# Bisecting the selection threshold in the float's own bits instead of ordered integers

## The chip, the cores and the metric

The kernel runs on one core of a Trainium2 chip. The metric is the time of one execution on the device, in microseconds (us); the median of several runs counts. The engines are TensorE (PE, with its weight loads as PEld), VectorE (DVE), ScalarE (ACT), GpSimd (POOL) and SyncE (SP), which here issues nearly all DMAs. Each engine works through its own queue in a fixed order and waits on semaphores for the others.

## The reference, cut to what matters

One decoder layer over 1024 tokens of width 1024: a norm, one wide projection, three token mixers (A: sparse attention, B: gated spatial MLP, C: differential attention), a gated merge, an output projection, and a feed-forward part with a final norm. The change touches A's choice of keys: each query keeps the 256 causal keys with the highest indexer score.

```python
score = jnp.einsum('bqh,bqhs->bqs', wb.astype(jnp.float32) * w_scale, jax.nn.relu(dots))
score = jnp.where(causal[None], score, -jnp.inf)
_, sel = lax.top_k(score, top_k)          # top_k = 256
...
logits = jnp.where(valid[:, :, None, :], logits, NEG)
p = jax.nn.softmax(logits, axis=-1).astype(v.dtype)
```

## The kernel before

Tokens are handled in eight tiles of 128 queries. Matmuls run as three products of a high and a low part (`mm`, line 84, over the pairs of `split_pairs`). The first phase, up to some 700 us, holds the projections, B, C, A and the gated merge; then come the output projection and the feed-forward part.

The indexer scores of tiles 2 to 7 lie in SBUF (`scA`, `scB`). No list of keys is built. Instead `selection` looks for each query's 256th highest score by bisection, bit by bit: 32 steps, each over all six tiles. A step makes a candidate threshold for every query and tile (128x6 values), counts in four tiles on VectorE (line 442, is_lt with a sum) and in the two largest on ScalarE (line 439, Sign with a sum), compares the counts with the goal (line 445) and takes the candidate where it holds (line 446, a predicated copy). Floats don't order like integers of the same bits when they are negative, so the candidate is kept as an ordered integer `K`, in which setting a bit makes it larger (line 432), and `to_float` turns it into the float's bits by a shift and mask (line 413) and an XOR (line 414):

```python
nc.vector.tensor_scalar(t, K, 31, INT_MAX, op0=ALU.arith_shift_right, op1=ALU.bitwise_and)
nc.vector.tensor_tensor(f, K, t, op=ALU.bitwise_xor)
```

After the last step the threshold above is tried (lines 453 to 471), and then six masks are made, one per tile (lines 484 to 493). A's softmax reads a mask for tiles 2 to 7; tiles 0 and 1 have a plain causal mask.

The work around it is written as generators that are advanced in turn. The projections of C take one selection step for each half of a product. Then a loop takes one half-step of `c_attention`, one step of `selection`, and one or two steps of `fill`, which holds B, A's projections, the gates of A, A's values (`proj_v`), and branches b and c. After C the selection is finished, then A runs with two steps of `fill` for each of its own. C works head by head (four heads): its Q and K come as two tiles each (`cQ`, `cK`) and V as one (`cV`), all from a ring of six places (tag `stk`), which A's `aQ`, `aK1`, `aK2`, `aV` use after them. C's score matmuls are line 576, its row minima on VectorE line 538, transposes line 510, value products line 525. A's scores are lines 795 and 796.

The order that an engine ends up with is not this order: the framework reorders each engine's queue by a simulated timeline when it builds the program, so a changed instruction can move others far away.

Of the kernel before, what the change touches and what calls it, by code (L numbers as in the profile page):

```python
# [12 lines left out]
I32 = mybir.dt.int32  # L13
AF = mybir.ActivationFunctionType
ALU = mybir.AluOpType

P = 128
# [9 lines left out]
INT_MIN = -(2 ** 31)  # L27
# [9 lines left out]
def trunk_kernel(tc, x, attn_g, w_in, ikg, ikb, sgug, sgub, sguw, sgubs, dlam, dsub,  # L37
                 wba, wbb, wbc, w_out, mlp_g, w_ff1, w_ff2, fin_g, out):
    nc = tc.nc
# [4 lines left out]
    with ExitStack() as top:  # L44
# [12 lines left out]
        def small(shape, name, bufs=4, dtype=F32):  # L57
            return spool[0].tile(shape, dtype, name=name, tag=name, bufs=bufs)
# [78 lines left out]
        with ExitStack() as ph:  # L137
# [61 lines left out]
            for i in range(NT):  # L199
# [3 lines left out]
                if i == 0:  # L203
# [7 lines left out]
                    for s in range(2):  # L211
# [4 lines left out]
                        for k0, kn, (H, L) in cv_parts:  # L216
                            a, b = max(k0, 4 * s), min(k0 + kn, 4 * s + 4)
# [94 lines left out]
            for i in range(NT):  # L312
                nc.vector.tensor_scalar(ikn[:, i, :], ikn[:, i, :], mv[:, i, 0:1], ikrs[:, i:i + 1],
                                        op0=ALU.subtract, op1=ALU.mult)
# [89 lines left out]
            NQ = len(QT)  # L404
# [3 lines left out]

            def to_float(K, tag):

                t = small([P, NQ], "selt", 2, I32)
                f = small([P, NQ], tag, 2, I32)
                nc.vector.tensor_scalar(t, K, 31, INT_MAX, op0=ALU.arith_shift_right, op1=ALU.bitwise_and)
                nc.vector.tensor_tensor(f, K, t, op=ALU.bitwise_xor)
                return f

            def sjunk(i):
                return (sja if i in ON_ACT else sjd)("junk")

            def selection():  # L420


                for a, i in enumerate(QT):
                    nc.vector.memset(thr[:, a:a + 1], float(P * (i + 1) - TOPK * (2 if i in ON_ACT else 1)))
                K = small([P, NQ], "selK", 1, I32)
                nc.vector.memset(K, INT_MIN)
                for b in range(31, -1, -1):
                    cand = small([P, NQ], "selc", 2, I32)
                    if b == 31:
                        nc.vector.memset(cand, 0)  # L430
                    else:
                        nc.vector.tensor_scalar(cand, K, 1 << b, None, op0=ALU.bitwise_or)
                    f = to_float(cand, "self")
                    cnt = small([P, NQ], "selcnt", 2)
                    for a, i in enumerate(QT):
                        junk = sjunk(i)
                        th = f[:, a:a + 1].bitcast(F32)
                        if i in ON_ACT:
                            nc.scalar.activation(junk[:, 0:P * (i + 1)], sc[i], AF.Sign, bias=th, scale=-1.0,
                                                 accum_out=cnt[:, a:a + 1])  # L440
                        else:
                            nc.vector.tensor_scalar(junk[:, 0:P * (i + 1)], sc[i], th, None,  # L442
                                                    op0=ALU.is_lt, op1=ALU.add, accum_out=cnt[:, a:a + 1])
                    ge = small([P, NQ], "selge", 2, I32)
                    nc.vector.tensor_tensor(ge, cnt, thr, op=ALU.is_le)
                    nc.vector.copy_predicated(K, ge, cand)
                    yield

                lo = small([P, NQ], "sello", 1, I32)
                hi_ = small([P, NQ], "selhi", 1, I32)  # L450
# [13 lines left out]
                for a, i in enumerate(QT):  # L464
                    if i in ON_ACT:
                        junk = sjunk(None)
                        nc.vector.tensor_scalar(junk[:, 0:P * (i + 1)], sc[i], f1[:, a:a + 1].bitcast(F32), None,
                                                op0=ALU.is_ge, op1=ALU.add, accum_out=cnt[:, a:a + 1])
                ge = small([P, NQ], "selge", 2, I32)
# [375 lines left out]
            def run_all(g):  # L845
                while next(g, 0) is None:
                    pass

            sel = selection()

            PER, count = 2, [0]
# [477 lines left out]
```

## Time and profile before

| | |
|---|---|
| median of 3 runs | 1477.47 us |
| lowest, highest | 1473.58, 1477.86 us |
| profiled execution | 1471.62 us |
| its span in the profile | 1469.9 us |
| mean granted clock of TensorE | 0.986 |
| busy: PE, PEld | 1414.8, 1195.9 us |
| busy: DVE, ACT, POOL | 998.6, 706.5, 566.7 us |

The profile is one execution. Busy times are those of the engine's instructions; matmuls are pipelined, so that a record lasts longer than the distance to the next, and their ends are modelled. The selection's counts run from 100 to 380 us, its masks until 440 us.

### The profile page before, as it was taken

The numbers are of one execution on the slowest core, as the hardware profiler recorded it, in microseconds if no ns is written. First come the engines' busy times: TensorE is split into PE (matmuls) and PEld (weight loads), VectorE is DVE, ScalarE is ACT, GpSimd is POOL, SyncE is SP. The second block draws the span as 40 slices with busy tenths as digits, with TensorE's granted clock in tenths as the row PEclk, the third lists the DMA queues.
The fourth block names the chain that finished last, engine by engine and source line by source line (L and its number), as shares of the span: only waits on it lengthen the run. The fifth ranks groups of instructions, "written<-read, shape, count | busy, mean of one in ns | idle before, by whom it ended". The sixth has DMA issues, their size and how long they took to land.

```text
span 1469.9 us, 20626 instructions
## 1 busy us (share of the span) xinstructions
PE 1414.8 (96%) x7257; PEld 1195.9 (81%) x7257; DVE 998.6 (68%) x2012; ACT 706.5 (48%) x1314; POOL 566.7 (39%) x373
## 2 busy tenths in 40 slices
PE   7999999998999999999999799999998699999997
PEld 6988888787978888887999578888887587888886
DVE  7478999999996644311615884444443799889795
ACT  6366667677533544422203565555544434334354
POOL 5102341112034323445522134444442557465574
PEclk9999999999999999999999899999999899999999
DMA  8446352535465657464633334444443944543522
GB/s 261 116 122 202 112 167 68 175 86 153 128 195 165 179 148 221 132 221 131 211 122 115 115 136 158 158 151 154 144 144 121 342 157 154 209 146 130 196 66 115
DMA packets 145344, 228.79 MB, mean 156 GB/s; under 512 B 16212, under 2 KB 79064, under 8 KB 145240
## 3 DMA queue, kind: packets, MB, share of 16 engines
q1 hardware_dynamic: 145240, 227.47, 47.7%
q8 instruction: 57, 0.93, 0.3%
q14 instruction: 47, 0.39, 0.1%
HBM read 152.46 MB, written 74.97 MB: 155 GB/s over the span
## 4 chain that ended last, share of the span: by engine, by line
PE 77%; DVE 12%; DMA 6%; issue 2%; ACT 1%; SPq 1%; POOL 0%; POOLq 0%; DVEq 0%; ACTq 0%
PE mm L84 29%; PE ff L1139 19%; PE fo L1292 17%; PE mm L994 4%; PE O L525 2%; DMA w2raw<-in_w_ff_dram 2%; DVE junk L442 2%; PE tp L510 1%; PE tp L994 1%; SPq L53 1%; DVE aS L1241 1%; DMA wr<-in_w_in_dram 1%; DVE cE L538 1%; DMA aK<-ak 1%; PE S L576 1%
## 5 line engine op out<-in xcount | busy, mean ns | idle before, releaser
L1292 PE MATMUL fo<-w2S,aS 128*128 128x512 f32 x1344 | 309.2, 392 | 18.0 <-ACT w2S L1240 15.5
L1139 PE MATMUL ff<-HS,WS 128*128 128x512 f32 x1344 | 312.0, 394 | 4.5 <-ACT WS L1020 1.6
L1292 PEld LDWEIGHTS fo<-w2S,aS 128*128 128x128 f32 x1344 | 254.1, 189 | 73.1 <-ACT w2S L1240 18.7
L1139 PEld LDWEIGHTS ff<-HS,WS 128*128 128x128 f32 x1344 | 253.3, 189 | 63.2 <-ACT WS L1020 2.4
L77 POOL TENSOR_TENSOR wl<-wr,wh 128x1024 fp32r<-128x1024 f32 x48 | 118.3, 2466 | 345.4 <-ACT wh L76 287.9
L84 PE MATMUL mm<-hH,wh 128*128 128x512 f32 (+1 forms) x544 | 214.3, 394 | 5.0 <-ACT gt L709 1.9
L84 PE MATMUL mm<-hH,wl 128*128 128x512 f32 (+1 forms) x544 | 212.6, 391 | 0.0
L84 PE MATMUL mm<-hL,wh 128*128 128x512 f32 (+1 forms) x544 | 212.2, 390 | 0.0
L1241 POOL TENSOR_TENSOR w2S<-w2raw,w2S 128x512 fp32r<-128x512 f32 x80 | 123.5, 1569 | 116.2 <-ACT w2S L1240 116.2
L1240 ACT CAST aS<-araw 128x512 fp32r<-128x512 f32 x112 | 62.5, 618 | 160.9 <-PE fo L1292 120.6
L1021 POOL TENSOR_TENSOR WS<-wraw,WS 128x1024 fp32r<-128x1024 f32 x35 | 85.2, 2435 | 138.8 <-ACT WS L1020 133.5
L1241 DVE TENSOR_TENSOR aS<-araw,aS 128x512 fp32r<-128x512 f32 x112 | 128.6, 1194 | 5.2 <-ACT aS L1240 5.2
L84 PEld LDWEIGHTS mm<-hH,wh 128*128 128x128 f32 x544 | 102.7, 189 | 26.3 <-ACT gt L709 3.4
L84 PEld LDWEIGHTS mm<-hH,wl 128*128 128x128 f32 x544 | 102.6, 189 | 19.9
L84 PEld LDWEIGHTS mm<-hL,wh 128*128 128x128 f32 x544 | 102.8, 189 | 18.6
L1296 DVE TENSOR_TENSOR x3b<-x3b,fo 128x512 f32<-128x512 f32 x168 | 106.7, 676 | 9.1 <-PE fo L1292 9.0
L76 ACT CAST wh<-wr 128x1024 fp32r<-128x1024 f32 x48 | 50.3, 1048 | 110.5 <-PE mm L84 47.0
L736 DVE SCALAR_TENSOR_TENSOR gt<-gt,mm 128x512 f32<-128x512 f32 x32 | 21.8, 683 | 72.5 <-PE mm L84 60.0
L544 ACT ACTIVATE cE<-cE,cEm 128x128 f32<-128x128 f32 (+7 forms) x64 | 49.6, 778 | 35.1 <-DVE cEm L541 18.8
L519 ACT CAST ptH<-tp 128x512 fp32r<-128x512 f32 (+1 forms) x80 | 42.6, 543 | 39.4 <-PE tp L510 31.9
L520 DVE TENSOR_TENSOR ptL<-tp,ptH 128x512 fp32r<-128x512 f32 (+1 forms) x80 | 50.2, 631 | 11.6 <-ACT ptH L519 10.1
L442 DVE TENSOR_SCALAR_CACHE_REDUCE junk<-scA,self 128x512 bf16<-128x512 f32 x64 | 55.8, 871 | 0.3
(309 smaller groups left out, 2873.6 us busy)
## 6 DMA issues: line engine op xcount, KB each, us to landing
wr<-in_w_in_dram SPq DMA_DIRECT2D x42, 512.0 KB, 4.6
araw<-a_s SPq DMA_DIRECT2D x28, 768.0 KB, 4.3
wraw<-in_w_ff_dram SPq DMA_DIRECT2D x16, 1024.0 KB, 5.3
a_s<-s SPq DMA_DIRECT2D x64, 256.0 KB, 2.0
a_s<-a SPq DMA_DIRECT2D x48, 256.0 KB, 2.3
w2raw<-in_w_ff_dram SPq DMA_DIRECT2D x8, 1536.0 KB, 8.0
araw<-a_s SPq DMA_DIRECT2D x14, 512.0 KB, 3.7
t_b<-gt SPq DMA_DIRECT2D x24, 256.0 KB, 2.9
```

What stands on the lines that cost most here:

```text
L76: nc.scalar.copy(H, raw)
L77: nc.gpsimd.tensor_tensor(L, raw, hi(H), op=ALU.subtract)
L84: nc.tensor.matmul(ps, st, mv, start=(i == 0), stop=(i == n - 1))
L442: nc.vector.tensor_scalar(junk[:, 0:P * (i + 1)], sc[i], th, None, op0=ALU.is_lt, op1=ALU.add, accum_out=cnt[:, a:a + 1])
L520: nc.vector.tensor_tensor(L[:, 0:w], tpf[:, 0:w], hi(H[:, 0:w]), op=ALU.subtract)
L994: nc.tensor.matmul(ps, st_, mv_, start=(kh == 0 and n_ == 0), stop=(kh == 1 and n_ == len(prs) - 1))
L1021: eng.tensor_tensor(W[:, 1], src, hi(W[:, 0]), op=ALU.subtract)
L1139: nc.tensor.matmul(ps, s_, mv_, start=(n in (1, 5, 2) and m_ == 0), stop=(m_ == len(prs) - 1), skip_group_check=True)
L1240: nc.scalar.copy(t[:, 0, i], s_[:, i])
L1241: eng.tensor_tensor(t[:, 1, i], s_[:, i], hi(t[:, 0, i]), op=ALU.subtract)
L1292: nc.tensor.matmul(ps, s_, mv_, start=(n in (1, 2, 5) and m_ == 0), stop=(m_ == len(prs) - 1), skip_group_check=True)
L1296: nc.vector.tensor_tensor(xs, xs, ps, op=ALU.add)
```

## The change

The threshold is kept as the float's own bits. The start is -1, all bits set, which is what `to_float` makes of the smallest integer. The first candidate is 0, as before. From then on the candidate of a bit is `K` XOR that bit: in a positive float the bit is set, which makes it larger; in a negative one, whose bits start all set, it is cleared, which makes it larger as well. Only after the 32 steps `to_float`, which is its own inverse, turns `K` into an ordered integer once, into a tile of its own (`selKo`), and the rest reads that. Of a step's six small instructions on VectorE two are no longer there; the counts now read the candidate `selc` and not `self`. Line numbers behind line 425 are higher by one, behind line 448 by two.

```diff
                 K = small([P, NQ], "selK", 1, I32)
-                nc.vector.memset(K, INT_MIN)
+                nc.vector.memset(K, -1)
                 for b in range(31, -1, -1):
-                    cand = small([P, NQ], "selc", 2, I32)
+                    f = small([P, NQ], "selc", 2, I32)
                     if b == 31:
-                        nc.vector.memset(cand, 0)
+                        nc.vector.memset(f, 0)
                     else:
-                        nc.vector.tensor_scalar(cand, K, 1 << b, None, op0=ALU.bitwise_or)
-                    f = to_float(cand, "self")
+
+                        nc.vector.tensor_scalar(f, K, 1 << b, None, op0=ALU.bitwise_xor)
                     cnt = small([P, NQ], "selcnt", 2)
...
                     nc.vector.tensor_tensor(ge, cnt, thr, op=ALU.is_le)
-                    nc.vector.copy_predicated(K, ge, cand)
+                    nc.vector.copy_predicated(K, ge, f)
                     yield
+                K = to_float(K, "selKo")
```

The build also moves other instructions. Three places:

VectorE, one of the first steps of the bisection, in the order before (`stL` is the low part of a projection, not of the selection):

```order
L445 TENSOR_TENSOR selge<-selcnt,selthr 128x6
L446 COPY_PREDICATED selK<-selge,selc 128x6
L432 TENSOR_SCALAR selc<-selK 128x6
L413 TENSOR_SCALAR selt<-selc 128x6
L345 TENSOR_TENSOR stL<-mm,stH 128x512
L414 TENSOR_TENSOR self<-selc,selt 128x6
L442 TENSOR_SCALAR junk,selcnt<-scB,self 128x384
L442 TENSOR_SCALAR junk,selcnt<-scA,self 128x512
```

The pair of lines 413 and 414 stands between the candidate and its counts. In the order of the changed kernel:

```order
L446 TENSOR_TENSOR selge<-selcnt,selthr 128x6
L447 COPY_PREDICATED selK<-selge,selc 128x6
L434 TENSOR_SCALAR selc<-selK 128x6
L443 TENSOR_SCALAR junk,selcnt<-scB,selc 128x384
L345 TENSOR_TENSOR stL<-mm,stH 128x512
L443 TENSOR_SCALAR junk,selcnt<-scA,selc 128x512
```

The two instructions of `to_float` are gone, and the first count follows the candidate directly.

SP, the loads for C's last head (heads are counted from 0, so head 3), in the order before: `wr` of 128x8x128 are a gate's weights, `wr` of 128x4x256 half of the weights for A's values, `t_a` and `o_s` are stores:

```order
L53 DMA o_s_1550<-ot 128x2x64
L53 DMA cK<-ck_1084 32x1024
L53 DMA cK<-ck_1085 32x1024
L53 DMA cQ<-cq_1080 32x1024 x2
L53 DMA cQ<-cq_1081 32x1024 x2
L53 DMA wr<-in_w_in_dram 128x8x128
L53 DMA wr<-in_w_branch_b_dram 128x2x128
L53 DMA wr<-in_w_in_dram 128x4x256
```

The gate's weights stand behind the C loads. In the changed kernel:

```order
L53 DMA t_a_77<-gt 128x512
L53 DMA wr<-in_w_branch_b_dram 128x2x128
L53 DMA wr<-in_w_in_dram 128x8x128
L53 DMA cK<-ck_1084 32x1024
L53 DMA cK<-ck_1085 32x1024
L53 DMA cK<-ck_1084 32x1024
L53 DMA cK<-ck_1085 32x1024
L53 DMA cQ<-cq_1080 32x1024 x2
L53 DMA cQ<-cq_1081 32x1024 x2
L53 DMA wr<-in_w_in_dram 128x4x256
```

The gate's weights stood behind the C loads and now stand in front of them; half of the weights for A's values takes the place behind.

TensorE, from the last score matmul of head 2 on, in the order before; the first row is the last that reads head 2's second Q tile, whose place in the ring the second K tile of head 3 takes (21 more matmuls of line 84, one of line 681 and two of line 600 follow before a score with that tile, 128x128):

```order
L576 MATMUL S_4383<-cK_3624,cQ_3623 128x512
L576 MATMUL S_4533<-cK_4510,cQ_4509 128x128
L525 MATMUL O_4144<-ptL_4164,cV_3633 128x256
L525 MATMUL O_4144<-ptH_4163,cV_3633 128x256
L525 MATMUL O_4144<-ptL_4164,cV_3633 128x256
L525 MATMUL O_4144<-ptH_4175,cV_3633 128x256
L525 MATMUL O_4144<-ptL_4176,cV_3633 128x256
L525 MATMUL O_4144<-ptH_4175,cV_3633 128x128
L525 MATMUL O_4144<-ptL_4176,cV_3633 128x128
L84 MATMUL mm_4738<-hH_110,wh_4610 128x512
L84 MATMUL mm_4738<-hL_112,wh_4610 128x512
L84 MATMUL mm_4738<-hH_110,wl_4611 128x512
```

A gate's product begins behind the value products. In the changed kernel, where the first row is the last reader of that place and the last row the first score with the new tile:

```order
L578 MATMUL S<-cK,cQ 128x512
L578 MATMUL S<-cK,cQ 128x128
L84 MATMUL mm<-hH,wl 128x512
L527 MATMUL O<-ptL,cV 128x256
L527 MATMUL O<-ptH,cV 128x256
L527 MATMUL O<-ptL,cV 128x256
L512 MATMUL tp<-ident,cE 128x128 x3
L683 MATMUL mm<-vn,wsT 128x256
L527 MATMUL O<-ptH,cV 128x256
L683 MATMUL mm<-vn,wsT 128x256 x2
L578 MATMUL S<-cK,cQ 128x128
```

The 24 matmuls of a gate's product no longer stand between the last reader and the new tile's first score.

## Rows read from the trace of the kernel before

**Rows 1.** Page, part 1: engine, busy us, share, instructions.
```profile
PE 1414.8 (96%) x7257; PEld 1195.9 (81%) x7257; DVE 998.6 (68%) x2012; ACT 706.5 (48%) x1314; POOL 566.7 (39%) x373
```

**Rows 2.** Busy time by stretches: us, then PE, PEld, DVE, ACT, POOL; clock, DMA share, GB/s.
```profile
106.00:441.00 335.00, 324.82 (x1854) 278.51 (x1852) 317.11 (x998) 213.29 (x445) 74.92 (x48) 0.99 0.49 142
...
441.00:634.00 193.00, 190.83 (x1011) 162.64 (x1010) 99.83 (x273) 85.91 (x182) 76.30 (x69) 1.00 0.54 164
```

**Rows 3.** Chain of waits: start us, duration us, what; two of its pieces.
```profile
320.43 0.60 PE tp L510 x4
...
855.00 277.01 PE ff L1139 x1210
```

**Rows 4.** TensorE groups by shape, 106 to 441 us; last what ended the idle time.
```profile
L84 PE MATMUL mm<-hH,wh 128*128 128x512 f32 x269 | 107.0, 398 | 5.0 <-ACT gt L709 1.9 <-DVE yt L691 1.6 <-DVE stL L345 1.1
...
L84 PE MATMUL mm<-wh,hH 128*128 128x256 f32 x192 | 55.0, 286 | 0.0
...
L510 PE MATMUL tp<-ident,cE 128*128 128x128 f32 x144 | 23.2, 277 | 0.0
...
L576 PE MATMUL S<-cK,cQ 128*128 128x512 f32 x48 | 18.8, 409 | 0.2 <-DVE cEm L538 0.2
...
L525 PE MATMUL O<-ptL,cV 128*128 128x256 f32 x64 | 18.0, 298 | 1.2 <-DVE ptL L520 1.0
```

**Rows 5.** VectorE groups, 106 to 441 us: line, shapes, count, busy us, mean ns, idle before.
```profile
L432 DVE TENSOR_SCALAR selc<-selK 128x6 int32<-128x6 int32 x31 | 7.4, 240 | 0.5
...
L414 DVE TENSOR_TENSOR self<-selc,selt 128x6 int32<-128x6 int32 x31 | 5.4, 174 | 0.5
...
L413 DVE TENSOR_SCALAR selt<-selc 128x6 int32<-128x6 int32 x31 | 5.2, 168 | 0.6
```

**Rows 6.** VectorE timeline of one step: start us, duration us, instruction.
```profile
245.11 0.17 DVE L413 TENSOR_SCALAR selt<-selc 128x6 int32<-128x6 int32 x1
...
245.31 0.17 DVE L414 TENSOR_TENSOR self<-selc,selt 128x6 int32<-128x6 int32 x1
...
246.05 0.16 DVE L586 RECIPROCAL cr<-cEs 128x1 f32<-128x1 f32 x1
...
246.13 0.40 DVE L646 SCALAR_TENSOR_TENSOR u<-gsq,mm 128x256 f32<-128x256 f32 x1
```

**Rows 7.** Chain of waits, start of the A stretch.
```profile
397.66 5.72 DMA aK<-ak
...
448.34 0.23 PE S L796
```

**Rows 8.** Chain of waits around the late weight.
```profile
326.64 6.14 DMA wr<-in_w_in_dram
...
334.71 7.20 PE mm L84 x24
```

**Rows 9.** TensorE timeline, 331 to 335 us; idle time and its releaser in brackets.
```profile
331.04 0.45 PE L576 MATMUL S<-cK,cQ 128*128 128x512 f32 x2
...
332.51 0.28 PE L525 MATMUL O<-ptL,cV 128*128 128x128 f32 x1
...
334.71 0.80 PE L84 MATMUL mm<-hH,wh 128*128 128x512 f32 x1 [1.92 <-ACT gt L709]
```

**Rows 10.** Stretch behind the late weight; columns as in rows 2.
```profile
334.70:338.10 3.40, 3.39 (x8) 2.71 (x9) 2.14 (x9) 3.37 (x9) 2.30 (x2) 0.53 0.86 257
```

**Rows 11.** SP timeline: the loads of head 3's second key.
```profile
331.46 1.72 SPq L53 DMA_DIRECT2D cK<-ck  x4
```

**Rows 12.** View of the tile cK: all its 32 loads.
```profile
DMA to landing us min/median/max: 2.3/3.2/5.5
```

**Rows 13.** VectorE groups of the masks, 385 to 441 us.
```profile
L488 DVE TENSOR_TENSOR_SCAN pf<-seleq,cm 128x384 f16<-128x384 bf16 (+5 forms) x6 | 10.0, 1663 | 0.0
...
L489 DVE SCALAR_TENSOR_TENSOR seleq<-pf,selneed,seleq 128x384 bf16<-128x384 f16 (+5 forms) x6 | 5.7, 948 | 0.1
```

## What was predicted

> **What bounds the kernel now.** I read the page first, then the busy time of each engine by stretches, then the groups of instructions inside the stretch that the change touches, then single places on the timeline and the chain of waits. The page says that TensorE is shown busy for 1414.8 of 1469.9 us and VectorE for 998.6 us [rows 1]. Taken over the whole span VectorE looks idle for a third of the time, but the change lies in one stretch, from the first candidate to the masks, 106 to 441 us. There VectorE is busy for 317.1 of 335 us, and TensorE for 324.8 [rows 2]. Behind that stretch VectorE falls to 99.8 of 193 us while TensorE stays at 190.8 [rows 2]. So in the stretch both engines are nearly full, and neither is free to give back what the other saves.
>
> TensorE's shown idle time of 10.2 us there is a lower bound, because the ends of matmuls are modelled. In the plain matmul run of the first feed-forward product 1210 matmuls of 512 columns take 277.01 us, 0.229 us each [rows 3]. In the stretch there are 856 of 512 columns (three groups of line 84, of which one is shown, and 48 scores) and 736 of 256 (three groups of line 84, 128 of line 525, 32 others) [rows 4]. At 0.229 us and half of that they need 196 and 84 us. The 144 records of transposes cost 0.15 us each by the chain, 21.6 us [rows 3, 4], and I allow 13 us for what is small. That is 315 of 335 us: an estimate of 20 us of gaps, 10.2 of them visible. These 20 us are all that this stretch can give, whatever VectorE saves.
>
> **The change part by part.** *The removed pair.* Each of the 32 steps loses a shift-and-mask (line 413) and an XOR (line 414); one pair of the 32 ran in the start-up, before VectorE had other work. The 31 pairs of the stretch are busy for 5.2 and 5.4 us, 10.6 us [rows 5]. Bounds: where the next instruction needs the result, the starts lie 0.20 us apart (245.11, 245.31), where it doesn't, about 0.08 us (246.05 to 246.13, a reciprocal) [rows 6]. 62 times these is 12.4 and 5.0 us. Since the scheduler puts other work between some of them and none between others, I take the 10.6 us.
>
> [...]
>
> *The OR that becomes an XOR* (line 432, 240 ns on average [rows 5]) keeps its form, one source and one constant on 128x6 integers: nothing. The memsets (-1 for the smallest integer) run in the start-up: nothing. *The conversion at the end* adds one pair behind the last step, 0.3 us at the same durations, taken once. Net for VectorE: 10.3 us less, so 306.8 of work for 335 us.
>
> *The moved instructions.* The order of every engine changes from the first C tiles on. Up to the second matmul of the first masked A score (448.34 us in the chain of before [rows 7]), VectorE has the same work as before less 62 instructions, two of them of the start-up and the new pair counted against the removed ones. But TensorE has 64 more 512-column matmuls in front of that place (1026 of line 84 against 962), 64 x 0.229 = 14.7 us of filling work that before stood behind it. On VectorE the six masks begin after 75 of the 96 C score chunks, not after 92, and end after 92, not after 96. So selection and masks go ahead of the last C tiles, and gates and projections on TensorE fill for them. The amount of TensorE work in the kernel stays the same, 7257 matmuls. So what the time can gain is only what gaps it loses.
>
> *The late weight.* On SP the load of a gate's weights stands behind C loads for the next head, which wait for tiles of the head in front: it is on its way from 326.64 for 6.14 us, and then it is copied and split [rows 8]. [...]
>
> *A new wait at the last head.* The tile of head 3's second key goes into the place of head 2's second query. In before that place is read last at 331.04 [rows 9], SP issues the four loads from 331.46 on for 1.72 us, and a load lands a median of 3.2 us after its issue, 2.3 to 5.5 [rows 11, 12]: ready some 4.9 us after the last read starts. TensorE's queue has 6.9 us of work between that last read and the first use (24 matmuls of 512 columns, seven value products and a few small ones), so nothing waits. In the new order 1.8 us of work stand there: one of 512 columns, a score of 128, seven of 256 and three transposes. So TensorE waits about 4.9 - 1.8 = 3.1 us. [...] By the same reckoning over all loads of Q, K and V tiles, the other short cover, 4.8 us for a key tile of A's third head, is the same in both orders.
>
> *VectorE's own part of the gaps.* In the rows of TensorE's groups [rows 4] 6.4 us of idle time stand (5.0, 1.2, 0.2), and VectorE ends 1.6, 1.1, 1.0 and 0.2 of it, 3.9 us or 61%; ScalarE's 1.9 is the late weight. The same share of 20 us is 12.2 us. VectorE's free time in the stretch goes from 17.9 to 28.2 us, and TensorE has 14.7 us of other work to put into what is left. I take two thirds, 8.1 us, as gained; bounds are 0 and 12.2.
>
> *What is late next.* In the A stretch 14.7 us of filling work are missing; it has 2.2 us of visible gaps in 193 us [rows 2]. I take a loss of 1.4 us there, with bounds 0 and 5.7, the length of one key load of A in the chain of before [rows 7]. TensorE's last 3834 of 7263 rows, from branch c on, stand in the same order as before.
>
> **Sum.** 8.1 + 3.6 - 4.8 - 1.4 = 5.5 us gained. The profiled execution took 1471.6 us (1469.9 of span and 1.7 around it), so 1466.1 by its own level. The median of the three runs shown is 1477.5, 5.9 us above it; at that level, which is the one that I give, the forecast is 1477.5 - 5.5 = 1472.0 us.
>
> **Rivals.**
> *TensorE stays the bound.* Both engines are in-order queues that feed each other, and TensorE has 315 of 335 us of work in the stretch. If its gaps come from the weaving (a transpose, a copy by ScalarE, a subtraction by VectorE, and back) and not from VectorE's load, VectorE merely gets idle time, as it has behind 441 us [rows 2]. For it: 94% use of TensorE in the stretch. Against it: VectorE is at 95% there and named for most visible gaps. The time is then between 1473 and 1481 us, about 1477.
>
> *The masks in front of the C tiles* (slower). The two costliest lines of the masks are busy for 15.7 us [rows 13], the six masks with all their lines for some 35. Before, they had nearly all of C behind them. Now the last 21 C chunks stand among and behind them in VectorE's queue, and TensorE's queue holds the transposes and value products of these tiles in a fixed place. TensorE's cover up to the last C score is 48 more matmuls of 512 columns (11.0 us) and 30 of 256 (3.4 us). If the masks' 35 us push C past that cover, TensorE waits 35 - 14 = 21 us; less the 5.5 that the forecast gains it is 15 us slower, 1493 us. It is slower by over 0.3% once TensorE waits more than 9.9 us there. Against it: the masks are interleaved chunk by chunk with C and not in one block, and waits of this sort, of TensorE on VectorE, are short in before, 1.0 us on the value products of line 525 [rows 4].
>
> *The pair is not removed, only renamed.* The built order has 3 of the 34 shift-and-masks left, so this gets hardly any chance.
>
> **How the numbers follow.** Changes below about 0.3%, 4.4 us, can't be told from none on this kernel. The forecast gets 0.58 and spans 2 to 18 us gained, 1459 to 1475; 0.55 of it lies past the 4.4 us and 0.03 short of them. TensorE as the bound gets 0.25, within 0.3% on either side. The masks get 0.15, all counted as slower. The renaming gets 0.02 (same). So faster 0.55; same 0.03 + 0.25 + 0.02 = 0.30; slower 0.15. The likeliest is 1472.0 us. Low end 1459: nearly all of the 20 us of gaps go, with no new wait. High end 1481: all of the bound's case. What is left out is some 0.04 below and 0.15 above.
>
> **What would show it.** VectorE's lines 413 and 414 fall from 34 instructions each to 3, and its busy time by about 10 us. In the stretch up to the first masked A score VectorE's busy share falls below 0.95, and TensorE's gaps shrink: the whole place should come at about the same time as before (441 to 450 us), with 64 more matmuls done. No gate weight should be waited for near 330 us, but TensorE should wait some 3 us for a key tile of head 3 at its first score with it. If the place comes at 455 us or later, TensorE was the bound. If TensorE waits at transposes of C's exponentials while VectorE runs lines 486 to 495, the masks' rival is right. The forecast is wrong, too, if the new order brings a new late load in the A stretch.

## The result and the profile of the changed kernel

The changed kernel is slower: 1488.15 us (median of six runs, 1485.29 to 1491.49) against 1474.93, ratio 1.0094 with an interval of 1.0075 to 1.0112. Timed again beside later experiments it took 1494.48 us, ratio 1.0136 (1.0115 to 1.0157). So it loses some 14 to 20 us where 5.5 were to be gained. The two timings of this one kernel lie 0.42% apart, 6.2 us, more than their intervals tell, so a difference of a few us between two experiments is safe only where the traces show it too. The profiled execution took 1489.2 us with a span of 1487.5.

Page of the changed kernel, part 1, as in [rows 1]:

```profile
PE 1420.3 (95%) x7257; PEld 1197.5 (81%) x7257; DVE 990.7 (67%) x1950; ACT 704.9 (47%) x1314; POOL 574.1 (39%) x373
```

Busy time by stretches, columns as in [rows 2]: the two stretches of before, and 3.4 us at a new wait.

```profile
106.00:441.00 335.00, 317.68 (x1797) 271.65 (x1796) 309.86 (x935) 208.00 (x438) 75.40 (x47) 0.99 0.49 140
441.00:634.00 193.00, 190.01 (x1002) 160.16 (x1001) 97.70 (x270) 84.64 (x181) 71.87 (x66) 1.00 0.55 163
340.40:343.80 3.40, 3.34 (x8) 2.67 (x9) 3.33 (x13) 1.75 (x6) 1.91 (x1) 0.53 0.97 254
```

VectorE works 7.9 us less in all. But between 106 and 441 us TensorE is busy for 317.7 us instead of 324.8. What it waits for there, and on to 500 us (engine and line, what was waited for, us in total, times, longest):

```profile
PE mm L84 <- DVE gv L648: 3.0, 1, 3.0
PE mm L84 <- DVE u L648: 1.9, 1, 1.9
PE S L578 <- DMA cV<-cvs: 1.9, 1, 1.9
PE mm L84 <- DVE gt L738: 1.7, 1, 1.7
PE O L527 <- DVE ptL L522: 1.6, 3, 0.8
PE mm L84 <- DVE selneed L488: 1.6, 1, 1.6
PE mm L683 <- DVE u L685: 1.4, 1, 1.4
PE mm L84 <- POOL wl L77: 1.2, 1, 1.2
```

In before the longest wait of this stretch was 1.92 us, for the late weight [rows 9]. Six of these eight lines are waits for VectorE, the engine that was relieved.

Where the time goes can be read from one long unbroken piece of TensorE's work near the end of each chain of waits: 1210 matmuls of the first feed-forward product, and the last 927 of the second. In the chain of the changed kernel (start us, duration us, what):

```profile
868.57 277.01 PE ff L1141 x1210
...
1266.15 210.88 PE fo L1294 x927
```

In before the first of them begins at 855.00 [rows 3], the second at 1247.88:

```profile
1247.88 212.47 PE fo L1292 x927
```

So the changed kernel is 13.6 us late before the feed-forward part, and loses 4.7 us more inside it, some 800 us behind the last instruction that was edited.

### The profile page after: what moved, and what is told of

It is laid out like the page before. It is cut to its first block, busy times and chain, and to the rows that moved or that the text cites. A ratio compares the mean times of both kernels' runs of the same rounds, so it can differ in the third digit from the quotient of the medians.

```text
span 1487.5 us, 20573 instructions
## 1 busy us (share of the span) xinstructions
PE 1420.3 (95%) x7257; PEld 1197.5 (81%) x7257; DVE 990.7 (67%) x1950; ACT 704.9 (47%) x1314; POOL 574.1 (39%) x373
## 4 chain that ended last, share of the span: by engine, by line
PE 70%; DVE 16%; DMA 6%; issue 4%; ACT 2%; POOL 1%; SPq 1%; POOLq 0%; DVEq 0%; ACTq 0%
PE mm L84 27%; PE ff L1141 19%; PE fo L1294 14%; PE mm L996 3%; DMA w2raw<-in_w_ff_dram 2%; DVE junk L443 2%; PE O L527 2%; DVE cE L540 2%; PE tp L512 1%; DVE aS L1243 1%; DMA wr<-in_w_in_dram 1%; DVE x3b L1298 1%; PE tp L996 1%; DVE cE L590 1%; DMA wr<-in_w_branch_c_dram 1%
## 5 line engine op out<-in xcount | busy, mean ns | idle before, releaser
L1294 PE MATMUL fo<-w2S,aS 128*128 128x512 f32 x1344 | 309.9, 393 | 20.4 <-ACT w2S L1242 14.9
L77 POOL TENSOR_TENSOR wl<-wr,wh 128x1024 fp32r<-128x1024 f32 x48 | 120.7, 2516 | 359.8 <-ACT wh L76 327.9
L1243 POOL TENSOR_TENSOR w2S<-w2raw,w2S 128x512 fp32r<-128x512 f32 x80 | 127.4, 1617 | 118.0 <-ACT w2S L1242 118.0
L84 PEld LDWEIGHTS mm<-hL,wh 128*128 128x128 f32 x544 | 103.0, 189 | 18.6
L84 PE MATMUL mm<-wh,hH 128*128 128x256 f32 x192 | 55.3, 288 | 4.5 <-DVE gv L648 3.0
```

The costliest lines, as they stand in the source:

```text
L77: nc.gpsimd.tensor_tensor(L, raw, hi(H), op=ALU.subtract)
L84: nc.tensor.matmul(ps, st, mv, start=(i == 0), stop=(i == n - 1))
L1243: eng.tensor_tensor(t[:, 1, i], s_[:, i], hi(t[:, 0, i]), op=ALU.subtract)
L1294: nc.tensor.matmul(ps, s_, mv_, start=(n in (1, 2, 5) and m_ == 0), stop=(m_ == len(prs) - 1), skip_group_check=True)
```

## The experiments

Two theories stood first. O: the rebuilt order of the queues costs the time. R: the removal itself does (counts that start earlier push other work back). To tell them apart a kernel needs one kernel's arithmetic and the other's order. This addition does that; the table `_ORDER` (left out here) holds, for each engine, the instructions by their place in the traced program, in the order wanted:

```python
for order in json.loads(zlib.decompress(base64.b64decode(_ORDER))).values():
    for a, b in zip(order, order[1:]):
        tc.add_manual_dep(ins[b], ins[a].name,
                          _mb.DependencyInfo(_mb.DependencyClass.NoSync, _mb.DependencyReason.DATA), reason="order")
```

These are order edges without a wait. "Order held" below means this.

**Changed arithmetic, order of before** (e1). The diff of the change, with the order held to that of before; the one conversion stands behind the last step.

> The changed arithmetic (32 pairs of small VectorE instructions gone, one pair added), with every engine's queue held in the order of the kernel before. Theory O (the rebuilt order costs the time): without the new order this is no slower than before; if VectorE's load is part of TensorE's gaps, as forecast, it gains some 8 us (1467), if TensorE is the bound it gains 0 to 3 us (1472 to 1475). Theory R (the removal itself costs: the counts start earlier and push other work of VectorE and ScalarE back): the order does not matter, and this takes what the changed kernel takes, about 1488 us.

Measured: 1470.40 us (12 runs), ratio 0.9968 (0.9954 to 0.9983). Theory R falls: in the order of before the removal gains 4.7 us, 0.32% of 1475. Its chain:

```profile
854.88 277.01 PE ff L1141 x1210
...
1247.12 210.88 PE fo L1294 x927
```

**Arithmetic of before, new order** (e2). No edit but the order, held to that of the changed kernel.

> The arithmetic of before (all 32 pairs), with every engine's queue held in the order of the changed kernel, each pair directly behind its candidate. Theory O: as slow as the changed kernel or somewhat slower, 1488 to 1496 us, since the 62 instructions (10.6 us of VectorE) come on top of the new order. Theory R: as fast as before, about 1475 us.

Measured: 1502.88 us, ratio 1.0188 (1.0162 to 1.0213). The order alone costs 28 us with the pairs in, and the pairs cost 8 to 15 us in it (against the two timings of the changed kernel). That is 7 us above the range expected, but Theory O stands.

**The pair twice, order of before** (e3).

```diff
                 nc.vector.tensor_tensor(f, K, t, op=ALU.bitwise_xor)
+                if tag == "self" and steps[0] < 32:
+                    steps[0] += 1
+                    nc.vector.tensor_scalar(t, K, 31, INT_MAX, op0=ALU.arith_shift_right, op1=ALU.bitwise_and)
+                    nc.vector.tensor_tensor(f, K, t, op=ALU.bitwise_xor)
                 return f
```

> Before, with the pair done twice in each of the 32 steps (64 instructions more, some 11 us of VectorE), every queue otherwise in the order of before. This is the price of the pair in a fixed order. If VectorE's load sets TensorE's gaps, as forecast: slower by 8 to 11 us, 1483 to 1486. If TensorE is the bound and VectorE's small instructions lie beside its work: within 3 us of before.

Measured: 1492.20 us, ratio 1.0123 (1.0101 to 1.0145): 18 us slower, 6 us above the higher of the two expectations. VectorE's busy time rises by more than the 11 us that were added, from 998.6 to 1019.3 us, since a few small instructions became much longer: the new lines 419 and 420 take 260 and 305 ns on average, the pair of before 168 and 174 [rows 5], while their medians are 172 and 166 ns and their longest 2.3 and 2.4 us. What these long ones fall together with is shown in the last section. TensorE's waits, 106 to 440 us:

```profile
PE O L531 <- DVE ptL L526: 5.1, 4, 2.7
PE mm L84 <- DVE gv L652: 3.6, 1, 3.6
PE S L582 <- DMA cK<-ck: 3.5, 1, 3.5
```

So in one and the same order 64 small instructions more cost 18 us and 62 fewer gain 5. VectorE's busy time goes up by 20.7 us in the one case and down by 5.0 in the other (993.6 us in e1); a second trace of before (e0) shows 1000.5, so a difference of 2 us says little.

**Short counts, order of before** (e5). On top of e1, VectorE's counts see only the first 128 keys, with a goal of 64. It leaves out the other keys of four tiles, so the masks are others.

```diff
-                    nc.vector.memset(thr[:, a:a + 1], float(P * (i + 1) - TOPK * (2 if i in ON_ACT else 1)))
+                    nc.vector.memset(thr[:, a:a + 1], float(P * (i + 1) - 2 * TOPK) if i in ON_ACT else 64.0)
...
-                            nc.vector.tensor_scalar(junk[:, 0:P * (i + 1)], sc[i], th, None,
+                            nc.vector.tensor_scalar(junk[:, 0:P], sc[i][:, 0:P], th, None,
```

> The changed arithmetic in the order of before, and VectorE's four counts of each step read only the first 128 keys instead of 384 to 768 (their goal is 64, so that the threshold is another and so is the output). That takes some 57 us of work from VectorE without moving an instruction. If VectorE's load set TensorE's gaps, as forecast (61% of 20 us): 8 to 12 us below the changed arithmetic in the order of before (1470), 1458 to 1462. If TensorE's gaps in this order come from the weaving of the queues: 0 to 4 us below, 1466 to 1470.

Measured: 1464.21 us, ratio 0.9935 (0.9914 to 0.9956), 4.9 us below e1 by the ratios. Its first feed-forward piece begins at 850.78 us, 4.1 before e1's. VectorE's busy time falls by another 59.9 us, to 933.7, and brings what the 5.0 of the pairs brought. Neither expectation is hit; the pairs and the shorter counts together, 65 us of VectorE's load, gave some 10 us, about half of the 20 us of gaps.

**Two sets of instructions moved up in VectorE's queue** (e4, e7). Each queue held, but in the new order five instructions, and in e1's order six, stand a few places earlier. The first of e4's five:

```
+L648 SCALAR_TENSOR_TENSOR gv<-gsq,mm 128x256
 L434 TENSOR_SCALAR selc<-selK 128x6
 L443 TENSOR_SCALAR junk,selcnt<-scB,selc 128x384
 L443 TENSOR_SCALAR junk,selcnt<-scA,selc 128x512
-L648 SCALAR_TENSOR_TENSOR gv<-gsq,mm 128x256
```

> The changed kernel in its own order, with five instructions moved up in VectorE's queue alone, each a few places: two of line 648 ahead of counts (line 443), one of line 685 ahead of two row minima and a predicated copy, one of line 252 ahead of a mask's scan (line 490), one of line 738 ahead of the small instruction of line 622. In the changed kernel TensorE waits for these five 3.0, 1.9, 1.4, 1.6 and 1.7 us, though their inputs are there earlier. Theory Q (the new order costs because VectorE's queue puts bulk in front of results that TensorE waits for): gains 3.0 + 1.6 + 0.8 + 1.5 + 1.7 = 8.6 us, 1479 to 1482. Theory S (VectorE is full in the new order, so that TensorE's waits only show its surplus of work): the waits come back at the next places, at most 3 us gained, 1485 to 1488.

Measured: 1492.70 us, ratio 1.0128 (1.0109 to 1.0148), above both ranges: nothing gained. The five waits are gone (lines 685 and 738, and 648 near 340 us) or shorter (0.3 and 0.9 us). Others stand at other places (e4's waits of TensorE, 106 to 500 us; the one for `selneed` is a new one, at 416 us):

```profile
PE O L527 <- ACT ptH L521: 3.7, 1, 3.7
PE mm L84 <- DVE selneed L488: 2.3, 1, 2.3
PE mm L84 <- DVE gv L648: 1.8, 2, 1.5
PE O L527 <- DVE ptL L522: 1.8, 3, 0.8
PE mm L84 <- DVE stL L345: 1.5, 2, 0.9
```

So a wait that can be seen is not a price that can be had back.

> The changed arithmetic in the order of before, with six instructions that TensorE waits for moved up by one or two places in VectorE's queue (lines 345, 693 twice, 685, 522, 599). The waits are 0.8, 0.5, 0.7, 0.8, 0.7 and 0.7 us. Theory Q: 3 to 4 us below the changed arithmetic in the order of before, 1466 to 1468. Theory S: no gain, 1470.

Measured: 1467.44 us (12 runs), ratio 0.9956 (0.9942 to 0.9970), 1.8 us below e1 by the ratios, within both intervals, so no gain over e1 is shown. It has the lowest median of the versions that leave nothing out, 0.44% below before.

**Short counts, new order** (e8). The edit of e5 on the changed kernel, order held to its own; it leaves out the same keys.

> The changed kernel in its own order, with VectorE's four counts of each step reading only the first 128 keys (goal 64, so that the threshold and the output are others): some 57 us less work for VectorE, no instruction moved. In the order of before the same edit gained 6 us. Theory S (the new order puts more VectorE work in front of the same TensorE work, so that VectorE is the bound up to the A stretch): most of the 18 us come back, 1465 to 1475. Rival (fixed waits of the new order: loads, the places in the queues): no more than the 6 us of the other order, 1482 to 1488.

Measured: 1484.49 us, ratio 1.0061 (1.0045 to 1.0077): 5 us below the changed kernel's first timing, 11 below its second. Theory S, that VectorE is simply too full up to the A stretch, falls as the sole cause. In e8's trace (of an execution of 1492.16 us, the slowest of its six) the wait for `gv` between 200 and 206 us is 0.3 us instead of 3.0, but those of the masks and the A stretch remain (lines 488, 685 and 738: 1.6, 1.4 and 1.7 us) with others beside them.

**The pace of the bisection** (e9, e10). In the changed kernel the 32nd step ends at 359.8 us, in e1 at 379.7 (end of the last step on VectorE, changed kernel, then e1):

```profile
359.82 0.17 DVE L447 COPY_PREDICATED selK<-selge,selc 128x6 int32<-128x6 int32 x1
```

```profile
379.72 0.15 DVE L447 COPY_PREDICATED selK<-selge,selc 128x6 int32<-128x6 int32 x1
```

The builder, given shorter steps, put them closer together: 74 of C's 96 row-minimum instructions of line 540 stand ahead of the end of the last step, 86 in before (line 538). e9 asks the builder for the old pace with 33 order edges on the changed kernel; e10 asks it for the new pace with 27 edges on the kernel before. For the changed kernel:

```diff
+    for later, earlier in _PACE:
+        tc.add_manual_dep(ins[later], ins[earlier].name,
+                          _mb.DependencyInfo(_mb.DependencyClass.NoSync, _mb.DependencyReason.DATA), reason="pace")
```

In each pair of `_PACE` (left out here) the later one is a candidate or a mask's first instruction, the earlier one a row minimum of C.

> The changed kernel, ordered by the framework anew, with 33 order edges and no table: 27 candidates of the bisection and six masks may not stand in VectorE's queue ahead of the row minimum of C (lines 540, 543) behind which they stood before. The bisection then ends behind 86 of the 144 row-minimum instructions, as before, and not behind 74. Theory P (it is the pace of the bisection against C that costs): 1468 to 1476, although this order is a third one, with 1718 of TensorE's 7249 instructions in other places than before. Rival D (any rebuilt order is a draw, and the pace has no part in it): anywhere from 1470 to 1495, as likely near 1488 as near 1472.

Measured: 1478.95 us (12 runs), ratio 1.0029 (1.0018 to 1.0040). Between the two: 10 to 16 us of the changed kernel's loss come back, 9 us remain against e1. It lies 3 us above the range of theory P and inside that of its rival D.

> The kernel before, with its 32 pairs, ordered by the framework anew with 27 order edges that make the bisection run ahead of C as it does in the changed kernel (its last step behind 74 row-minimum instructions instead of 86). The masks are not held. Theory P: slower than before by 10 to 28 us, 1485 to 1503 (the same arithmetic in the very order of the changed kernel took 1503). Rival D: near 1475, as before.

Measured: 1491.61 us, ratio 1.0115 (1.0102 to 1.0128). A few edges, and not one instruction more or less, cost before 17 us, as theory P expected. But the builder made a whole new order in both cases, so the two don't set the pace apart from all else that moved; every order that it rebuilt here (the changed kernel, e9, e10) was slower than that of before. The trace of e10 shows the wait for `gv` that the changed kernel has (TensorE timeline):

```profile
199.10 0.52 PE L84 MATMUL mm<-wh,hH 128*128 128x256 f32 x1 [3.04 <-DVE gv L646]
```

**Which stretch of the new order costs** (e11 to e14, e16, e17). The orders are joined: all that starts before a moment stands in one order, the rest in the other.

> The changed arithmetic in the new order for all that starts up to 344 us in the changed kernel's trace (30 of the 32 steps), and in the order of before for the rest. If the parts add up: 8 us above the changed arithmetic in the order of before (1470), 1477 to 1480. If the bisection's part is given back later: 1470 to 1473.

Measured: 1477.30 us (12 runs), ratio 1.0024 (1.0007 to 1.0041), 8.3 us above e1 by the ratios. Its chain has the 1210 matmuls 7.8 us later than e1, so the bisection's part is not given back:

```profile
862.64 277.00 PE ff L1141 x1210
...
1255.97 210.85 PE fo L1294 x927
```

> The changed arithmetic in the order of before for all that starts up to 334 us (26 steps), then in the new order up to the feed-forward part, which has the order of before. If the parts add up: 5 to 6 us above 1470, 1475 to 1477. If the second part costs only because the first has left VectorE behind: 1470 to 1472.

Measured: 1495.31 us, ratio 1.0152, some 18 us above its range. Spoilt by its seam: right behind it TensorE waits 10.98 us for line 648, because VectorE first has to catch up four steps.

> The changed arithmetic in the new order for all that starts up to 470 us of the changed kernel's trace (the bisection, the masks and the first part of the A stretch), then the order of before. The new order up to 344 us alone took 1477 us. If the masks' part costs 4 to 6 us by itself: 1481 to 1484, and the rest up to the changed kernel's time is the A stretch's end and the feed-forward part. If the masks cost nothing: 1477.

Measured: 1499.88 us, ratio 1.0179, 16 us above its range. Spoilt as well: TensorE waits five times, 1.1 to 2.1 us, for line 626 between 471 and 491 us, where no other kernel waits for it. So the masks' part wasn't measured alone.

> The changed kernel in its own order, but the feed-forward part (lines above 990) of every queue in the order of before: 22 places on TensorE, 13 on VectorE, 9 on ScalarE. If the waits of 0.8, 1.8 and 0.8 us for aS near 1215, 1239 and 1266 us come from VectorE's new order there: 3 to 5 us below the changed kernel, 1483 to 1485. If they are a matter of when the loads land: 1488.

Measured: 1486.76 us, ratio 1.0087 (1.0068 to 1.0106), 1.0 us below the first timing of the changed kernel by the ratios, less than expected. To settle it the same kernel and the changed kernel were timed side by side (e16, e15):

> The changed kernel, timed beside the next two. Two single executions of it and of its near copy took 1490 to 1495 us, the six of the first timing 1485 to 1491: expected 1486 to 1493.

> The changed kernel with the feed-forward part in the order of before, as in the run before of the same kernel. In that trace the three waits for aS were gone and TensorE was 4 to 6 us earlier behind them: 3 to 5 us below the changed kernel of the same job. If they are made up for elsewhere: the same time.

Measured: 1494.48 and 1487.15 us, ratios 1.0136 and 1.0088 (1.0062 to 1.0114), the first 1.5 us above its range: 7.1 us by the ratios, with intervals that all but touch (1.0114, 1.0115). Then the tail alone:

> The changed arithmetic in the order of before, with the feed-forward part (lines above 990) alone in the new order: 22 places on TensorE, 13 on VectorE, 9 on ScalarE. If these cost by themselves: 4 to 7 us above 1470, 1474 to 1477, with waits of some 0.8, 1.8 and 0.8 us for aS near 1200, 1224 and 1250 us. If they only cost behind a late first part: 1470.

Measured: 1476.89 us (12 runs), ratio 1.0018 (1.0007 to 1.0030), 7.4 us above e1, clear of both intervals. Its chain:

```profile
854.14 276.99 PE ff L1141 x1210
...
1254.56 210.89 PE fo L1294 x927
```

The first piece begins like e1's, the second 7.4 us later. All traces of these orders agree: from the start of the first piece to that of the second it is 392.2 to 394.9 us in the eleven with the old order of the feed-forward part (before, e0, e1, e3, e5, e7, e11 to e14, e16) and 397.6 to 400.5 in the seven with the new one (the changed kernel, e2, e4, e6, e8, e15, e17). What is swapped there on VectorE is the adding-up of the second product (line 1298, which needs TensorE's result) against the split of its next operand (line 1243, which TensorE needs), from the order of before (-) to that of the changed kernel (+):

```
 L1298 TENSOR_TENSOR x3b_11699<-x3b_11699,fo 128x512
+L1298 TENSOR_TENSOR x3b_11700<-x3b_11700,fo 128x512
+L1243 TENSOR_TENSOR aS<-araw,aS 128x512 x2
+L1298 TENSOR_TENSOR x3b_11701<-x3b_11701,fo 128x512
 L1243 TENSOR_TENSOR aS<-araw,aS 128x512
-L1298 TENSOR_TENSOR x3b_11700<-x3b_11700,fo 128x512
+L1298 TENSOR_TENSOR x3b_11702<-x3b_11702,fo 128x512
 L1243 TENSOR_TENSOR aS<-araw,aS 128x512
-L1298 TENSOR_TENSOR x3b_11701<-x3b_11701,fo 128x512
-L1243 TENSOR_TENSOR aS<-araw,aS 128x512 x2
-L1298 TENSOR_TENSOR x3b_11702<-x3b_11702,fo 128x512
 L1298 TENSOR_TENSOR x3b_11703<-x3b_11703,fo 128x512
```

Each sum now stands one place or two nearer the front, so that VectorE waits for more of TensorE's product before it makes the next operand. In e17 TensorE waits 2.6 us for `aS` and 3.8 for `x3b` between 1170 and 1300 us, in e1 2.4 us for `x3b` alone:

```profile
PE fo L1294 <- DVE x3b L1298: 3.8, 3, 2.2
PE fo L1294 <- ACT aS L1242: 2.6, 2, 1.8
```

```profile
PE fo L1294 <- DVE x3b L1298: 2.4, 1, 2.4
```

These waits are only the end of it. The swap stands near 1168 to 1176 us and leaves VectorE 1.9 us later there. SyncE loads `araw`, which line 1243 reads, and behind it in its queue the next weights (`w2raw`); it waits for line 1243 to free the places, so the weights come later too. Two pieces of each chain of waits, e1 and then e17:

```profile
1203.34 2.90 DVE aS L1243 x2
...
1206.63 8.98 DMA w2raw<-in_w_ff_dram
```

```profile
1209.58 2.32 DVE aS L1243 x2
...
1212.28 9.44 DMA w2raw<-in_w_ff_dram
```

The load is issued 5.7 us later, and VectorE stands idle for it for 4.54 us (line 1231, at 1221.82), in e1 for 2.25 (at 1215.71). The 1.9 us have grown to 5.7 mostly because the eight subtractions of line 1243 in front, which fall beside GpSimd's own subtractions more often there, take 11 us in e17 and 7 in e1. Of the 112 such subtractions in the changed kernel, 32 overlap with none of GpSimd's (same line) and take 0.68 us in the median; 49 lie at least nine tenths inside GpSimd's and take 1.58.

**Second traces** (e0 of before, e6 of the changed kernel).

> The kernel before, unchanged, for a second trace of it: which of TensorE's waits come back at the same place with the same length, and which change from one execution to the next. Expected: 1470 to 1478 us; the waits of the first 700 us at the same places within 0.5 us each, the waits in the second feed-forward product (line 1292) at other places.

> The changed kernel, unchanged, for a second trace. Expected: 1485 to 1491 us, the waits up to 700 us at the same places within 0.5 us each; if the extra waits of the second feed-forward product near 1240 to 1260 us (some 5 us against the order of before) belong to one execution, they are not there again or stand elsewhere.

Measured: 1470.76 and 1494.43 us; the second is 3.4 us above its range. Both have nearly all of their own waits again at the same places, those of the feed-forward part too, which was not expected of before, so these don't belong to one execution. Single waits differ by up to 2 us where 0.5 were expected: the one for `gv` near 205 us is 3.0 us in the changed kernel's first trace and 0.9 in e6. In its time up to the first feed-forward piece the new order also varies more: 864.0 to 872.9 us in five traces (the changed kernel, e6, e11, e15, e16), 854.1 to 855.6 in four of the old order (before, e0, e1, e17).

## How the queues lock: two places

Changed kernel, VectorE, 199 to 206 us (start us, duration us, instruction, in brackets idle time before and its releaser):

```profile
201.49 0.29 DVE L540 CUSTOM_DVE_ANT_0 cE<-S,cm 128x128 f32<-128x128 f32 x1 [1.13 <-PE S L578]
...
201.70 2.23 DVE L434 TENSOR_SCALAR selc<-selK 128x6 int32<-128x6 int32 x1
203.96 0.61 DVE L443 TENSOR_SCALAR_CACHE_REDUCE junk<-scB,selc 128x384 bf16<-128x384 f32 x1
...
204.62 0.75 DVE L443 TENSOR_SCALAR_CACHE_REDUCE junk<-scA,selc 128x512 bf16<-128x512 f32 x1
...
205.29 0.42 DVE L648 SCALAR_TENSOR_TENSOR gv<-gsq,mm 128x256 f32<-128x256 f32 x1
```

and TensorE in the same time:

```profile
201.15 0.59 PE L578 MATMUL S<-cK,cQ 128*128 128x128 f32 x3 [0.58 <-issue]
...
205.76 0.38 PE L84 MATMUL mm<-wh,hH 128*128 128x256 f32 x1 [2.98 <-DVE gv L648]
```

VectorE waits 1.13 us for a score of TensorE, then does the next candidate and two counts, and only then frees the product that TensorE waits for. Both queues are right by themselves; woven in this order each waits for the other in turn. But most of these 2.98 us is the candidate, which takes 2.23 us here. In e6, the same kernel in the same order, it takes 0.17 and the wait is 0.91 us:

```profile
199.69 0.17 DVE L434 TENSOR_SCALAR selc<-selK 128x6 int32<-128x6 int32 x1
...
200.36 2.38 POOL L77 TENSOR_TENSOR wl<-wr,wh 128x1024 fp32r<-128x1024 f32 x1 [4.01 <-ACT wh L76]
...
201.69 0.39 PE L84 MATMUL mm<-wh,hH 128*128 128x256 f32 x1 [0.91 <-DVE gv L648]
```

The other traces of this order split in the same way: 0.9 us in e11 and e16, where the candidate is short, 2.5 to 2.9 in e12, e14 and e15, where it is long. So some 0.9 us of this wait is the order's, and 2.1 come from the long instruction, on which the last section has more. The wait of 3.04 us in e10 has such a one in front of it as well (line 413, 2.13 us at 196.52).

The same in the feed-forward part, changed kernel, VectorE:

```profile
1233.41 1.76 DVE L1231 TENSOR_TENSOR T1b<-w2raw 128x1536 f32<-128x1536 f32 x1 [4.57 <-DMA w2raw<-in_w_ff_dram]
1235.09 0.68 DVE L1298 TENSOR_TENSOR x3b<-x3b,fo 128x512 f32<-128x512 f32 x1
1235.69 2.88 DVE L1243 TENSOR_TENSOR aS<-araw,aS 128x512 fp32r<-128x512 f32 x2
1238.49 2.47 DVE L1298 TENSOR_TENSOR x3b<-x3b,fo 128x512 f32<-128x512 f32 x4
```

VectorE stands idle for 4.57 us until the late weights land, so the sum (line 1298) and the low part of `aS` (line 1243) come behind them. TensorE's next matmul, which reads `aS`, begins at 1239.31 after 1.82 us of waiting. The wait is put down to ScalarE's high part of `aS` (line 1242, from 1237.52), which had itself waited 2.28 us for TensorE's matmuls in front.

Behind the masks the new order has nothing left for VectorE. Busy time for the same amount of TensorE's work (its columns from some 110 us on, summed up from its rows), changed kernel and then e1:

```profile
111.00:433.00 322.00, 304.68 (x1737) 260.78 (x1736) 303.88 (x924) 202.40 (x430) 75.40 (x47) 0.99 0.48 139
433.00:470.00 37.00, 37.00 (x183) 30.61 (x182) 8.01 (x21) 10.99 (x22) 6.18 (x4) 1.00 0.43 120
```

```profile
110.00:419.00 309.00, 301.20 (x1748) 259.82 (x1747) 289.50 (x912) 206.16 (x435) 69.22 (x46) 1.00 0.49 140
419.00:458.00 39.00, 37.51 (x179) 30.30 (x178) 31.87 (x59) 10.44 (x22) 15.78 (x12) 1.00 0.57 175
```

VectorE has 303.9 us of work in front of that point instead of 289.5, with the pairs gone in both, and 8.0 instead of 31.9 behind it. The builder pulled later work in front, and TensorE came 13 us later to the same point. That the one is the reason for the other was not tested alone; e8 took some 55 us of VectorE's work out of this order and gained 5 to 11.

## Why the prediction was wrong

- **The moved instructions** are the step that failed. I priced three places: 3.6 gained (the late weight), 4.8 (the last head) and 1.4 (the A stretch) lost, 2.6 us lost in sum. Measured, the new order costs 1.26% (first timing against e1) to 1.68% (second), 18.6 to 24.8 us. Of it 8.3 us stand in the bisection (e12), 7.4 in the feed-forward part (e17); if the parts add up, the rest, 3 to 9 us, falls to the masks and the A stretch, where the trace of the changed kernel loses 5.9 us (13.7 late at the first feed-forward product against e1, less 7.8 in e12). That last share was not measured alone.
- **"TensorE's last 3834 of 7263 rows, from branch c on, stand in the same order as before"** was true only of rows without buffer numbers. With them 22 places differ, and VectorE's queue, which I had not followed to the end, differs in 13. These few cost 7.4 us by themselves (e17), more than the 4.7 that the removal gains.
- **"VectorE's free time in the stretch goes from 17.9 to 28.2 us"** took the work of the stretch as given. Between 106 and 441 us VectorE is busy for 309.9 of 335 us, 25.1 free, so the number nearly came true; but TensorE had got less far by then. In front of the same TensorE work VectorE had 14.4 us more to do than in e1: the builder moved work there. I had seen that the masks begin after 75 instead of 92 chunks, and read the 64 matmuls in front as filler for TensorE instead of as VectorE's work come earlier.
- **The removed pair.** The lines fell from 34 to 3 each, as said. In a fixed order the removal gains 4.7 us (2.5 to 6.8 by the interval) where the term said 8.1, with bounds of 0 and 12.2: right in kind and within the bounds, too large by 3.4. The 10.6 us taken out shortened VectorE's busy time by 5.0 only (6.9 against e0); the candidate became longer (299 ns on average in e1, two of 31 at 2.0 and 2.2 us; its median is 171 ns with the OR in before and 168 with the XOR in the changed kernel). Of the 20 us of gaps some 10 came back with 65 us of VectorE's load taken out (e5).
- **The late weight.** The wait for it is gone, but the next product of that kind waits 1.9 us for line 648 at 340 us, and the granted clock behind it is 0.53 over 3.4 us (340.4 to 343.8 us, above), as in before [rows 10]. So no run shows the sum's 3.6 us for it; what stands in its place is as long, and about nothing is gained.
- **The new wait at the last head** is there, but smaller: 0.46 us at 353 us in the changed kernel's first trace, 1.9 in e6, below 0.3 in e15, where 3.1 were forecast. Nor does a run show the sum's 4.8 us for it: the longest of these waits is the 1.9 us, and behind the one of 0.46 the granted clock is 1.00 (353.4 to 356.8 us). TensorE is held by VectorE just ahead of it (line 685, 1.4 us), which gives the load time.
- **The rivals.** "Masks in front of the C tiles" gave the sign and nearly the time, 1493 us, with 0.15. Its mechanism exists (1.6 us for line 252 behind a mask's scan, line 490; the view of waits names the instruction after it, line 488), but 15.7 us of the cost stand elsewhere, so the sign came out for another reason and the time by luck. "TensorE stays the bound" has its sign, a first masked A score at 455 us or later:

```profile
473.62 0.40 PE L798 MATMUL S<-aK,aQ 128*128 128x512 f32 x1
```

That is 25 us later than in before, and only 14.7 of them are the 64 matmuls moved in front. Its time, 1473 to 1481 us, is missed, and TensorE, busy for 7.1 us less in the stretch, was late and not full. Beyond the masks no rival covered an order that is worse in itself; 0.55 for faster rested on the removed work and the late weight alone.

## What to carry to other kernels

When a builder orders the queues, an edit has two parts: what it does to the work, and a new order. Price them apart by holding the order; here, where the two busiest engines of the stretch were both over 94% busy in before [rows 2], the second part was several times the first (19 to 25 us lost against 5 gained). Compare the queues of every engine to the program's end, with buffer numbers, and keep the old order where the new one is worse: with it this change gains 0.32%. Before a wait is put down to the order, look in a second trace whether it has the same length.

## What the runs showed of the hardware

An instruction on 128x6 elements that mostly takes 0.17 us (line 434) took 2.23 us at 201.70 us (above). GpSimd ran one long instruction in just that time, changed kernel, GpSimd:

```profile
201.54 2.35 POOL L77 TENSOR_TENSOR wl<-wr,wh 128x1024 fp32r<-128x1024 f32 x1 [4.02 <-ACT wh L76]
```

VectorE's instruction ends within 0.1 us of it. In e6 the candidate had ended before GpSimd's instruction began (above), and was short.

Counted over all twenty traces the pattern holds. Taken are VectorE's instructions on 128x6 integers (arithmetic, comparison, predicated copy) and those on 128x1 with two tensors that begin inside one of these GpSimd subtractions of 128x1024, 0.25 us or more before its end. There are 291. Of these 280 end within 0.04 us of its end; the 11 that keep their usual 0.15 us all begin within 0.1 us of its start. Of 112 reciprocals on 128x1 that begin inside one, none takes over 0.3 us. So in these traces it went by the sort of instruction and not by its size. The cause was not tested by a run of its own.

Which instruction it falls on changes with the order, and from one execution to the next, so the mean of a small instruction is no fixed price: the candidate's line took 240 ns on average in before [rows 5] and 318 in the changed kernel. In e3 thirteen small instructions between 106 and 441 us take over 1 us, 25.0 us above their usual length in sum; in before it is eight with 13.4. With the 11 us of the pairs this accounts for the 20.7 us by which VectorE's busy time rose.
